# Three local edits in a seven-product block multiply: when a 2.3 MB load is issued, when one weight split stands in its queue, and which bank one product gets

## The chip, the cores and the metric

The kernel runs on one core of one Trainium2 chip. The metric is the device time of one execution in microseconds (us). Before the change the median of three runs is 2394.07 us (2391.72 to 2394.24). The engines are named as in the profile: PE multiplies matrices, PEld is its weight load, DVE is the vector engine, ACT the scalar engine, POOL is GpSimd, and SP issues most of the DMAs. The built program holds one list of instructions for each engine, with waits on semaphores that the others raise; the trace shows each list carried out in its order.

## The reference, cut to what matters

One layer of an encoder trunk is computed for 512 prompt frames and 64 sample frames, so 576 columns, which the kernel handles as two halves of 288 columns:

```python
proj = rmsnorm(x) @ w_in                  # 2048 -> 6144: q, k, v, gb, gc, hc
o_attn = stick_breaking(q, k, v)          # 8 heads
o_conv = gb * conv3(gc * hc)              # 1024 channels, 8 groups of 128
x = x + concat(rmsnorm(o_attn), rmsnorm(o_conv)) @ w_out
x = x + (silu(h2 @ w_gate) * (h2 @ w_up)) @ w_down     # h2 = rmsnorm(x); 5632 wide
```

Everything is in float32. The kernel multiplies in a rounded form (fp32r), so each operand is split into a high part and a low part, and each product is made of three matmuls: high x high, low x high and high x low, with the weights' part named first.

## The kernel before, in words

**Seven products.** Most of the large multiplies are blocked two by two: the inner dimension in even and odd chunks, the output channels in two groups c = 0, 1, the frames in two halves i = 0, 1. The four output blocks (c, i) come from seven products instead of eight, numbered 1 to 7 here as in the code, written (n, p) for product p of unit n. Each product is 24 matmuls of 128x288 (8 chunks by three). The sums and differences of weights that the products need are made by DVE in place, those of the frames beforehand: for products 5, 6, 7 and 4 of the convolution's units they lie in DRAM as `xs_dram[0..3]`. Products 1, 6, 5 and 3 of a unit accumulate one after another in one PSUM bank (`psy`), 7 and 4 in another (`psw`), and 2 has its own (`psx`). What is in `psy` after product 1, 6 and 5 is needed by itself, so ACT copies it out each time (`kept`, L1591 in the units of the second part, L1044 in the first) before the next product may go on adding to the bank. Block (1, 1) is `psw` after product 7 plus the copy after product 5; block (0, 1) is `psy` after product 3; block (1, 0) is `psw` after product 4 plus the copy after product 6.

**The order.** PE's order is written out by hand in two lists. `corder` (L1155) is for the convolution's units and the attention's share of the output projection: it begins (0,1), (0,2), (1,1), (1,2), (0,7), (0,6), (0,5), (0,3), (0,4), (1,6), (1,7), (1,5), and then (2,1), (1,3), (1,4). `order` (L1502) is for the gate, up and down units: it begins (0,1), (0,2), (1,1), (1,2), (0,6), (0,7), (0,5), (0,3), (0,4). So in the first list unit 0 already differs from the others, and there the fifth product of unit 0 has a bank of its own (L1083 to L1091): ACT copies it out (L1088), POOL adds the earlier copy to it (L1090), DVE makes block (1, 1) from `psw` and that sum (L1059, then a multiply by the row scale R, L1061), and block (0, 1) is `psy` plus the copied fifth product.

**Weights.** `conv_prepare(n, p)` (L975) makes one product's weights: DVE forms the sum if one is due (L993, L997, L1006, L1010, L1011), ACT writes the high part (L1004, 128x1024), DVE subtracts it for the low part (L1007, 128x1024). In the second part `prepare` does the same with the helper at L223 and L224, and the sums at L1526 to L1532. Four weight buffers are in turn, so a product's weights can be made up to four products ahead. `begin` (L1171) says after which products of `corder` the first weights are prepared: the entry with index k_ lists the places in `corder` whose weights are made after place k_ has run. Up to place 8 the orders of ACT and DVE are those of the program text; behind it, a scheduler of the tile framework orders them when the program is built.

**Loads at the start of the convolution's units.** SP's queue carries, in this order: the stores of the attention's forms (`form_dram<-hf`, L553), the eight loads of `xs_dram[0]` into the tiles `x` (L1152, 288 KB each), one load of weight columns (`raw_a`, L970, called from `conv_prepare` once a place is free: it holds the second column group of unit 1), the load of `xs_dram[3]` into `xs_t` (`load_sum`, L861, 2304 KB, called after place 2 of `corder`), and two more loads of weight columns. The tile of `xs_t` takes the memory of `hf`. `xs_t` is what product (0,4) multiplies; the sums for products 6 and 7 were loaded earlier, `x` serves product 5.

**Evictions.** `conv_run` (L1039) runs a product and then lets DVE make what blocks are complete: after product 2, `done` (L1047) adds the copy of product 1 to `psx` (L1059) and multiplies by R (L1061). Product 2 of units 0 and 1 use one bank, `z0`. In the second part `run` (L1585) and `finish` (L1394) do the same for gate and up: an add (L1404), a multiply by R (L1405), and for the gate a Silu on ACT (L1407); a block without an added part takes the multiply alone (L1402).

Of the kernel before, what the change touches and what calls it, by code (L numbers as in the profile page):

```python
# [10 lines left out]
F32 = mybir.dt.float32  # L11
F32R = mybir.dt.float32r
AF = mybir.ActivationFunctionType
ALU = mybir.AluOpType
PSUM = bass.MemoryType.PSUM

P = 128
# [3 lines left out]
HALF = T // 2  # L21
# [73 lines left out]
def tile_hybrid_stream_step(  # L95
# [6 lines left out]
    nc = tc.nc  # L102
# [14 lines left out]
    tmp = ctx.enter_context(tc.tile_pool(name="tmp", bufs=2, side="left"))  # L117
# [63 lines left out]
    def load_weight():  # L181
        i = len(raws)
        raws[i], raw3, src = weight_raw(i)
        nc.sync.dma_start(out=raw3, in_=src)

    def split_weight(lo_eng):
        raw = raws[len(ready)]
        n = specs[len(ready)][1] * specs[len(ready)][2]
        hi, lo = weight_split(len(ready))
        for a in range(0, n, 1024):  # L190
            weight_parts(raw, hi, lo, a, a + 1024, lo_eng)
# [69 lines left out]
    def misc(name):  # L261
        return ps_z.tile([P, 512], F32, tag="misc", name=name, bufs=2)
# [111 lines left out]
    with tc.manual_schedule(engines={mybir.EngineType.Activation, mybir.EngineType.DVE, mybir.EngineType.SP}):  # L374
# [26 lines left out]
        for kt in range(KD + LAG):  # L401
# [21 lines left out]
            if kt == 16:  # L423
                nc.vector.tensor_tensor(out=lo1[:, :1024], in0=raws[1][:, :1024], in1=hi1[:, :1024].bitcast(F32),  # L424
                                        op=ALU.subtract)
# [58 lines left out]
    for i in range(5):  # L484
        n = P if i < 4 else TS
# [373 lines left out]
    def load_sum(q):  # L859
        t = bt[q] = bt["pool"].tile([P, NP, 2, HALF], F32R, tag=f"t{q}", name=f"xs_t{q}")  # L860
        nc.sync.dma_start(out=t.bitcast(F32), in_=xs_dram[q].rearrange("j f p t -> p j f t"))  # L861

    def open_units():
        cx = apool.tile([P, 1024 + UW + 2 * HALF], F32, tag="ob", name="cx")
        bt["mx"] = cx[:, 1024 + UW :].rearrange("p (f t) -> p f t", t=HALF).bitcast(F32R)
        bt["s1"] = cx[:, :1024].rearrange("p (j c) -> p j c", c=P)
        bt["c"] = cx[:, 1024 : 1024 + UW - 2]
# [239 lines left out]
    def load_forms(tile_, at, f):  # L1107
        ft[f] = tile_[:, at : at + NH // 2]
        nc.sync.dma_start(out=ft[f].bitcast(F32), in_=form_dram[f - 1].rearrange("j f p t -> p j f t"))

    def open_out():

        xpool.release()
        bt["y"] = ypool = tc.alloc_tile_pool(name="ypool", bufs=1, reuse_waits="tile", side="right")
        x2t.extend(ypool.tile([P, 2, T], F32, tag=f"y{j}", name=f"x2_{j}") for j in range(NP))
        bt["m"] = tc.alloc_tile_pool(name="mpool", bufs=1, reuse_waits="tile", side="right")
        bt["mc"] = bt["m"].tile([P, 2, NG, 2, HALF], F32R, name="mixc")
        bt["R"] = rpool.tile([P, T], F32, tag="R", name="R_c", bufs=2)
        pipe.spawn(load_rest())
        pipe.spawn(state_out())  # L1120
        pipe.spawn(group_scale(bt["acc"], bt["R"], 7), 7 * 28)
# [6 lines left out]
    def add_x(d):  # L1128
        nc.gpsimd.dma_start(out=x2t[d], in_=xt_dram[2 * d : 2 * d + 2].rearrange("k p t -> p k t"), accum_op=ALU.add)
# [21 lines left out]
    for j in range(NP):  # L1151
        nc.sync.dma_start(out=xt[j][:, 0, 1].bitcast(F32), in_=xs_dram[0, j].rearrange("f p t -> p f t"))  # L1152
    pipe.flush()
    open_units()
    corder = [(0, 1), (0, 2), (1, 1), (1, 2), (0, 7), (0, 6), (0, 5), (0, 3), (0, 4), (1, 6), (1, 7), (1, 5)]  # L1155
    for n in range(2, len(CU)):
# [11 lines left out]
            corder += [(n, 1), (n - 1, 3), (n - 1, 4), (n, 2), (n, 6), (n, 7), (n, 5)]  # L1168


    begin = [(), (3, 4), (5,), (6, 7), (8,), (), (9,), (10, 11), (12,)]  # L1171
    turn_mode = ExitStack()
    for k_, (n, p_) in enumerate(corder):
        if (n, p_) == (NCU - 1, 1):
            turn_mode.enter_context(tc.manual_schedule(engines={mybir.EngineType.SP}))
        if k_ == len(begin) - 1:
            start_mode.close()
        conv_run(n, p_)
        for q in begin[k_] if k_ < len(begin) else range(k_ + 4, min(k_ + 5, len(corder))):
            conv_prepare(*corder[q])  # L1180
        if k_ == 2:
            load_sum(3)
        if n == NCU - 1 and p_ in (6, 7, 4):
            q = {6: 1, 7: 2, 4: 3}[p_]
            t = bt["pool"].tile([P, NH, 2, HALF], F32R, tag=f"t{q}", name=f"forms{q}")
            for at, f in enumerate({1: (1, 2), 2: (6, 7), 3: (5, 3)}[q]):
                load_forms(t, 4 * at, f)
            if p_ == 7:
                load_forms(apool.tile([P, NH // 2, 2, HALF], F32R, tag="oa", name="forms0"), 0, 4)
        if (n, p_) == (NCU - 1, 3):  # L1190
            open_out()
        if n >= NCU and p_ == (3 if n < NCU + 2 or n == len(CU) - 1 else 4):
            add_x(n - NCU)
        if k_ in (len(corder) - 10, len(corder) - 5):
            load_weight()
        if k_ == len(corder) - 4:
            split_weight(nc.vector)
# [292 lines left out]
    def frames(n, p_):  # L1490

        kind, _, a, m = UNITS[n]
        if kind == "down":
            return [(slots[a + j][p_ - 1][:, 0, :], slots[a + j][p_ - 1][:, 1, :]) for j in range(m)]
        if p_ < 3:
            return h2a[p_ - 1 :: 2]
        if p_ == 3:
            return b22s
        return [(frame_sum(p_, j, 0), frame_sum(p_, j, 1)) for j in range(m)]
# [77 lines left out]
    def multiply(ps, n, p_, start):  # L1577
        whl, xs_ = operand.pop((n, p_)), frames(n, p_)
        for j, (xh, xl) in enumerate(xs_):
            for q, (w_, x_) in enumerate(((0, xh), (1, xh), (0, xl))):  # L1580
                mm(ps, whl[:, w_, j, :], x_, start=(start and j == 0 and q == 0),  # L1581
                   stop=(j == len(xs_) - 1 and q == 2), skip_group_check=True)
            pipe.tick()

    def run(n, p_):  # L1585
        st = unit[n]
        kind, fp = UNITS[n][:2]

        def kept(tag):
            t = tmp.tile([P, HALF], F32, tag=tag, name="part", bufs=1)  # L1590
            nc.scalar.copy(out=t, in_=st["y"])  # L1591
            return t

        def done(c, i, ps, part=None):
            if kind != "down":
                finish(kind, fp, c, i, ps, part)
            elif n in last:
                store_y(n, c, i)

        def add(c, i, ps, part=None):  # L1600

            if kind != "down":
                return
            if n in first:
                if part is not None:
                    nc.vector.tensor_tensor(out=acc[fp, c, i], in0=ps, in1=part, op=ALU.add)
                else:
                    nc.scalar.copy(out=acc[fp, c, i], in_=ps)
                return
            if ps is not None:  # L1610
                nc.vector.tensor_tensor(out=acc[fp, c, i], in0=ps, in1=acc[fp, c, i], op=ALU.add)
            if part is not None:
                nc.gpsimd.tensor_tensor(out=acc[fp, c, i], in0=acc[fp, c, i], in1=part, op=ALU.add)

        if kind == "down" and p_ == 1 and n in first:
            take_blocks(fp)
        later = n not in first
        if p_ == 1:
            st["y"] = ps_pj.tile([P, HALF], F32, tag="pj", name="psy")
            multiply(st["y"], n, 1, True)  # L1620
            st["p1"] = kept("ms")
        elif p_ == 2:
            x = ps_z.tile([P, 512], F32, tag="z0", name="psx2")[:, :HALF]
            multiply(x, n, 2, True)
            add(0, 0, x, st["p1"])
            done(0, 0, x, st["p1"])
        elif p_ == 6:
            multiply(st["y"], n, 6, False)
            st["u2"] = kept("ms" if n == NGU - 1 else "t")
            if later:  # L1630
                add(1, 0, None, st["u2"])
        elif p_ == 7:
            st["w"] = ps_z.tile([P, 512], F32, tag=f"z{n % 2 + 1}", name="psw")[:, :HALF]
            multiply(st["w"], n, 7, True)
            if later:
                add(1, 1, st["w"])
        elif p_ == 5:
            multiply(st["y"], n, 5, False)
            u4 = kept("acc")
            add(1, 1, None if later else st["w"], u4)  # L1640
            done(1, 1, st["w"], u4)
        elif p_ == 3:
            multiply(st["y"], n, 3, False)
            add(0, 1, st["y"])
            done(0, 1, st["y"])
        else:
            multiply(st["w"], n, 4, False)
            add(1, 0, st["w"], None if later else st["u2"])
            done(1, 0, st["w"], st["u2"])
# [6 lines left out]
    for d, v in visits.items():  # L1656
        n = next(a for a, b in zip(v, v[1:]) if a >= NGU + 10 and b >= a + 4)
        residual.setdefault(n + 1, []).append(d)
    acc = {}
# [190 lines left out]
```

## Time and profile before

| | us |
|---|---|
| median of three runs | 2394.07 (2391.72 to 2394.24) |
| the profiled execution, device time | 2392.95 |
| its span, first to last instruction | 2391.2 |
| PE busy in the span | 2368.7 |
| DVE busy | 1902.1 |
| ACT busy | 1165.2 |
| POOL busy | 289.1 |

All times below are counted from the start of the span; what lies around it is 2392.95 - 2391.2 = 1.75 us. A row of the timeline gives the start, the duration, the engine, the line of the kernel, the operation, the output and its inputs, and the count of instructions that were merged; in square brackets stands how long the engine had been idle before, and what released it. A row of 24 matmuls is one product. Durations of matmul rows contain a tail of about 0.16 us that overlaps the next row, so products are best counted from start to start. A row of the waits says who waited for whom, the total, how often, and the longest. A row of the windows gives a stretch, its length, each engine's busy time and number of instructions, the granted share of PE's clock, the busy share of the DMA engines, and GB/s. A row of DMA issues gives the queue, the count, the size of each, and the median time from issue to landing.

### The profile page before, as it was taken

To read this page: it belongs to the slowest core of one execution; us is meant where nothing else is said; L and a number is where in the kernel's file an instruction comes from. 1 tells how busy PE (TensorE), PEld (TensorE's weight loads), DVE (VectorE), ACT (ScalarE), POOL (GpSimd) and SP (SyncE) were. 2 spreads that over 40 slices of the span, in tenths; PEclk is the share of its full clock that TensorE was granted. 3 is DMA by queue.
4 is the path that set the end of the run, shared out by engine and by line. 5 is a ranking of instruction groups with operands and counts; after the bars stand their busy time and mean duration, and the time that the engine had idled before them with its cause. 6 is when DMAs were issued, how large, how long until landed. Compare 5 with 4: busy or idle time off the path is not lost.

```text
span 2391.2 us, 44089 instructions
## 1 busy us (share of the span) xinstructions
PE 2368.7 (99%) x17813; PEld 2358.7 (99%) x17813; DVE 1902.1 (80%) x2855; ACT 1165.2 (49%) x2087; POOL 289.1 (12%) x385
## 2 busy tenths in 40 slices
PE   8999999999999999999999999999999999999999
PEld 8999999999999999999999999999999999999998
DVE  7867776688887768888888888888888777977875
ACT  6666665444444545444444444444444444444444
POOL 1111111241121120000000000000000002431211
PEclk9999999999999999999999999999999999999999
DMA  7354433584367643435534534434444935885642
GB/s 256 116 149 144 144 112 96 190 278 126 108 215 199 206 138 116 145 119 156 157 110 156 160 114 157 151 123 148 151 132 145 342 130 197 227 233 197 201 132 81
DMA packets 503764, 386.04 MB, mean 161 GB/s; under 512 B 11534, under 2 KB 492680, under 8 KB 503560
## 3 DMA queue, kind: packets, MB, share of 16 engines
q1 hardware_dynamic: 494216, 366.68, 47.9%
q0 software_dynamic: 8624, 16.22, 3.3%
q8 instruction: 139, 2.28, 0.4%
q14 instruction: 65, 0.53, 0.1%
q10 hardware_dynamic: 720, 0.33, 0.0%
HBM read 296.47 MB, written 86.72 MB: 160 GB/s over the span
## 4 chain that ended last, share of the span: by engine, by line
PE 90%; DVE 4%; DMA 3%; ACT 2%; issue 1%; POOL 0%; SPq 0%; ACTq 0%; DVEq 0%; POOLq 0%
PE psy L1581 34%; PE psw L1581 17%; PE pj L214 11%; PE psx L1581 8%; PE psy L1035 6%; PE pjo L214 4%; PE psw L1035 3%; PE pw L1424 2%; PE psx L1035 1%; DMA raw_a<-in_w_out_dram 1%; PE z L684 1%; DMA xs_t<-xs_dram 1%; PE po L751 0%; DVE wlo L177 0%; DVE whl L1007 0%
## 5 line engine op out<-in xcount | busy, mean ns | idle before, releaser
L1581 PE MATMUL psy<-t,whl 128*128 128x288 f32 x2916 | 438.0, 295 | 0.0
L1581 PE MATMUL psy<-h_s,whl 128*128 128x288 f32 x2724 | 410.9, 294 | 0.0
L1581 PEld LDWEIGHTS psy<-t,whl 128*128 128x128 f32 x2916 | 403.4, 188 | 0.0
L214 PE MATMUL pj<-x,whi 128*128 128x288 f32 x1856 | 398.9, 299 | 0.3 <-DVE x L357 0.3
L1581 PEld LDWEIGHTS psy<-h_s,whl 128*128 128x128 f32 x2724 | 377.9, 188 | 0.3 <-ACT part L1591 0.3
L1581 PE MATMUL psw<-t,whl 128*128 128x288 f32 x2592 | 377.0, 295 | 0.0
L224 DVE TENSOR_TENSOR whl<-raw_a,whl 128x1024 fp32r<-128x1024 f32 (+4 forms) x288 | 313.4, 1089 | 58.9 <-ACT whl L223 57.9
L1581 PEld LDWEIGHTS psw<-t,whl 128*128 128x128 f32 x2592 | 354.1, 188 | 0.0
L223 ACT CAST whl<-raw_a 128x1024 fp32r<-128x1024 f32 (+4 forms) x288 | 259.5, 902 | 118.1 <-issue 35.4
L214 PEld LDWEIGHTS pj<-x,whi 128*128 128x128 f32 x1856 | 307.3, 189 | 1.0 <-DVE x L357 0.6
L214 PE MATMUL pj<-x,wlo 128*128 128x288 f32 x928 | 274.5, 296 | 0.1
L224 DVE TENSOR_TENSOR whl<-raw_b,whl 128x1024 fp32r<-128x1024 f32 (+5 forms) x186 | 194.4, 1045 | 69.7 <-ACT whl L223 68.5
L223 ACT CAST whl<-raw_b 128x1024 fp32r<-128x1024 f32 (+5 forms) x186 | 161.0, 868 | 162.1 <-issue 69.9
L1591 ACT COPY part<-psy 128x288 f32<-128x288 f32 x237 | 94.5, 399 | 272.5 <-PE psy L1581 271.3
L214 PEld LDWEIGHTS pj<-x,wlo 128*128 128x128 f32 x928 | 175.2, 189 | 0.7 <-DVE wlo L424 0.3
L1581 PE MATMUL psx<-h_s,whl 128*128 128x288 f32 x1122 | 165.0, 295 | 0.0
L1581 PEld LDWEIGHTS psx<-h_s,whl 128*128 128x128 f32 x1122 | 154.1, 188 | 0.0
L1339 POOL DMA_DIRECT2D hid_dram<-form x3 | 2.2, 748 | 975.7 <-DVE form L224 975.7
L223 ACT CAST whl<-s 128x1024 fp32r<-128x1024 f32 (+5 forms) x79 | 70.1, 888 | 98.9 <-PE psw L1581 97.3
L177 DVE TENSOR_TENSOR wlo<-raw_a,whi 128x1024 fp32r<-128x1024 f32 (+1 forms) x80 | 96.6, 1224 | 10.1 <-ACT whi L176 8.0
L214 PE MATMUL pjo<-mixc,whi 128*128 128x288 f32 x512 | 101.7, 294 | 0.0
L176 ACT CAST whi<-raw_a 128x1024 fp32r<-128x1024 f32 (+1 forms) x85 | 85.6, 1024 | 29.4 <-PE pj L214 15.6
(469 smaller groups left out, 4114.9 us busy)
## 6 DMA issues: line engine op xcount, KB each, us to landing
hid_dram<-form SPq DMA_DIRECT2D x146, 288.0 KB, 2.3
raw_a<-in_w_in_dram SPq DMA_DIRECT2D x41, 1024.0 KB, 6.9
raw_a<-in_w_gate_dram SPq DMA_DIRECT2D x23, 1024.0 KB, 5.9
raw_a<-in_w_up_dram SPq DMA_DIRECT2D x23, 1024.0 KB, 5.9
raw_b<-in_w_gate_dram SPq DMA_DIRECT2D x21, 1024.0 KB, 6.7
raw_b<-in_w_up_dram SPq DMA_DIRECT2D x21, 1024.0 KB, 7.5
h_s<-hid_dram SPq DMA_DIRECT2D x10, 2016.0 KB, 8.5
raw_a<-in_w_out_dram SPq DMA_DIRECT2D x16, 1024.0 KB, 5.2
```

Source lines behind the costliest of these rows:

```text
L176: nc.scalar.copy(out=hi[:, a:b], in_=raw[:, a:b])
L177: lo_eng.tensor_tensor(out=lo[:, a:b], in0=raw[:, a:b], in1=hi[:, a:b].bitcast(F32), op=ALU.subtract)
L214: mm(ps, w_[:, k, csl], x_, start=(k == 0 and n == 0), stop=(k == nk - 1 and n == 2))
L223: nc.scalar.copy(out=hi, in_=src)
L224: (lo_eng or nc.vector).tensor_tensor(out=lo, in0=src, in1=hi.bitcast(F32), op=ALU.subtract)
L684: mm(zb[i], a_[:, kk], b_[:, q0:TP], start=(n == 0), stop=False, skip_group_check=True)
L1035: mm(ps, whl[:, w_, j, :], x_, start=(start and j == 0 and q == 0), stop=(j == m - 1 and q == 2), skip_group_check=True)
L1339: q.dma_start(out=hid_dram[fp][2 * n - 2 : 2 * n].rearrange("f p t -> p f t"), in_=t.bitcast(F32))
L1424: mm(pss[j, i], w_[:, k, j * P : (j + 1) * P], x_, start=(kk == 0 and k == 0 and n == 0), stop=(kk == 1 and k == 7 and n == 2))
L1581: mm(ps, whl[:, w_, j, :], x_, start=(start and j == 0 and q == 0), stop=(j == len(xs_) - 1 and q == 2), skip_group_check=True)
L1591: nc.scalar.copy(out=t, in_=st["y"])
```

## The change: what it does

- `load_sum(3)`, the load of `xs_dram[3]` into `xs_t`, is called before the units begin, directly behind the eight loads of `xs_dram[0]`, instead of after place 2 of `corder`.
- The weights of (1,2), place 3 of `corder`, are prepared after product (0,1) instead of after (0,2), so their split stands ahead of the eviction of (0,2) in the queues. Those of (0,7) stay where they were.
- In the first gate unit (unit 0 of the second part) the fifth product gets a bank of its own. ACT copies it out, POOL adds the copy of product 6 to it for block (1, 1), and block (0, 1) is `psy` plus the copied fifth product.

```diff
     pipe.flush()
+    load_sum(3)
     open_units()
...
-    begin = [(), (3, 4), (5,), (6, 7), (8,), (), (9,), (10, 11), (12,)]
+    begin = [(3,), (4,), (5,), (6, 7), (8,), (), (9,), (10, 11), (12,)]
...
         for q in begin[k_] if k_ < len(begin) else range(k_ + 4, min(k_ + 5, len(corder))):
             conv_prepare(*corder[q])
-        if k_ == 2:
-            load_sum(3)
...
+        elif p_ == 5 and n == 0:
+
+            x = misc("psx5")[:, :HALF]
+            multiply(x, n, 5, True)
+            st["p5"] = tmp.tile([P, HALF], F32, tag="acc", name="part5", bufs=1)
+            nc.scalar.copy(out=st["p5"], in_=x)
+            u4 = tmp.tile([P, HALF], F32, tag="ms", name="part", bufs=1)
+            nc.gpsimd.tensor_tensor(out=u4, in0=st["p5"], in1=st["u2"], op=ALU.add)
+            done(1, 1, st["w"], u4)
         elif p_ == 5:
             multiply(st["y"], n, 5, False)
...
         elif p_ == 3:
             multiply(st["y"], n, 3, False)
             add(0, 1, st["y"])
-            done(0, 1, st["y"])
+            done(0, 1, st["y"], st.get("p5"))
```

When the two programs are built, every engine's instructions stand in the same order up to the start of the convolution's units. From there, on SP `xs_t` moves ahead of one `raw_a` load. On DVE the L1007 of (1,2) moves ahead of the L1059 and L1061 of (0,2). Behind place 8 the scheduler's order of DVE and ACT differs in some places up to the middle of the units: above all, both evictions that belong to (0,3) and (0,4) stand directly behind the low part of (1,6), and on ACT the copy of (1,6) and the convolution's first tap (L890) stand ahead of the high part of (1,5). In the gate unit one POOL add, one DVE add and other names are the only differences.

## The prediction

> **What bounds the kernel now.** I read the totals first, then what PE waited for, then the timeline at those waits.
>
> ```profile
> PE 2368.7 (99%) x17813; PEld 2358.7 (99%) x17813; DVE 1902.1 (80%) x2855; ACT 1165.2 (49%) x2087; POOL 289.1 (12%) x385
> ...
> PE psw L1035 <- DMA xs_t<-xs_dram: 3.4, 1, 3.4
> ...
> PE psy L1581 <- ACT part L1591: 1.4, 1, 1.4
> ...
> PE psx L1035 <- DVE whl L1007: 0.9, 1, 0.9
> ```
>
> PE is busy 99% of 2391.2 us; only what shortens its few waits can help. Each edit aims at one of these three: 5.7 us together. The first costs more than its wait:
>
> ```profile
> 513.26 1.22 DVE L1007 TENSOR_TENSOR whl<-raw_a,whl 128x1024 fp32r<-128x1024 f32 x1
> 514.54 3.07 PEld L1035 LDWEIGHTS psw<-xs_t,whl 128*128 128x128 f32 x23 [0.37 <-DVE whl L1007]
> ...
> 520.86 3.33 PE L1035 MATMUL psx<-x,whl 128*128 128x288 f32 x24
> 524.03 3.33 PE L1035 MATMUL psy<-x,whl 128*128 128x288 f32 x24
> 530.73 4.95 PE L1035 MATMUL psw<-xs_t,whl 128*128 128x288 f32 x24 [3.37 <-DMA xs_t<-xs_dram]
> 535.52 3.37 PE L1035 MATMUL psy<-xs_t,whl 128*128 128x288 f32 x24
> 528.00:532.00 4.00, 1.27 (x6) 1.30 (x7) 2.80 (x4) 1.99 (x2) 0.00 (x0) 0.87 1.12 361
> 532.00:536.00 4.00, 4.00 (x24) 4.00 (x23) 2.09 (x5) 0.24 (x1) 1.39 (x2) 0.71 0.15 43
> ```
>
> The first two rows are the low part of (0,7) and PE's weight loads waiting for it; the PE rows below are (0,5), (0,3), (0,4), (1,6). A product takes 3.17 us start to start (520.86 to 524.03). From (0,3) to (1,6) there are two products, 6.34, but the trace has 535.52 - 524.03 = 11.49. So the late `xs_t` costs **5.15 us**: 3.53 until (0,4) starts, and 1.62 because it then runs at a granted clock of 0.87 and 0.71.
>
> **Part 1, the load of `xs_t`: removes 5.15.**
>
> ```profile
> 506.51 4.56 SPq L1152 DMA_DIRECT2D x<-xs_dram  x8
> 518.11 0.37 SPq L970 DMA_DIRECT2D raw_a<-in_w_in_dram  x1
> 518.54 1.92 SPq L861 DMA_DIRECT2D xs_t<-xs_dram  x1
> 516.00:518.00 2.00, 2.00 (x17) 2.00 (x17) 1.97 (x2) 1.06 (x1) 0.00 (x0) 1.00 0.24 84
> 520.00:530.60 10.60, 7.36 (x56) 7.12 (x54) 6.17 (x8) 2.62 (x5) 0.80 (x1) 1.00 1.08 347
> xs_t<-xs_dram SPq DMA_DIRECT2D x1, 2304.0 KB, 12.1
> ```
>
> Before, `xs_t` stood in SP's queue behind a `raw_a` load that waited until 518.11 for DVE. Now it follows the eight `x` loads, at 506.51 + 4.56 = 511.1. Those keep the DMA engines busy until about 517 (84 GB/s in 516 to 518, so they are running dry). 2304 KB (2.36 MB) at the 347 GB/s of the busy stretch is 6.8 us, so `xs_t` lands near 523.8. (0,4) wants it at 524.03 + 3.17 = 527.2 or later: the wait and the slow clock go. The old DMA gap around 518 hides the move. Also on SP's queue, the `raw_a` of (1,6) is now behind `xs_t`: 1.05 MB more, 3.0 us, 526.8. Who needs that is below.
>
> **Part 2, the split moved up: adds 0.9.**
>
> ```profile
> 508.58 1.05 ACT L1004 CAST whl<-raw_c 128x1024 fp32r<-128x1024 f32 x1
> 508.71 0.46 DVE L1059 TENSOR_TENSOR cv<-psx,part 128x288 f32<-128x288 f32 x1
> 509.20 0.46 DVE L1061 TENSOR_TENSOR cv<-cv,R 128x288 f32<-128x288 f32 x1
> 509.66 1.23 DVE L1007 TENSOR_TENSOR whl<-raw_c,whl 128x1024 fp32r<-128x1024 f32 x1
> 510.80 1.22 DVE L993 TENSOR_TENSOR raw_a<-raw_a 128x1024 f32<-128x1024 f32 x1
> 510.94 3.33 PE L1035 MATMUL psx<-x,whl 128*128 128x288 f32 x23 [0.86 <-DVE whl L1007]
> ```
>
> (1,2) waited for its low part. That in turn started 0.03 after ACT's high part ended (508.58 + 1.05 = 509.63). ACT's order is unchanged here, so the L1007 can't start earlier; it has only moved ahead of L1059 and L1061, which used DVE while ACT was still at work. DVE now idles until 509.66, and the two follow at 510.80. Two things wait for that. (1,2) uses bank `z0`, so its first matmul waits until L1059 has read it: 510.80 + 0.46 = 511.26, some 0.5 later than now. And L993 and all behind it come later by what the pair took, 509.66 - 508.71 = 0.95, less about 0.1 of overlap: 0.9 (estimate). The first to feel it is (0,7), which already waits for its low part (0.37 above): that ends at 515.4 instead of 514.5. (0,7) thus starts its stream 0.9 later, the 0.5 included. Were ACT's cast earlier, up to the 0.86 would be won instead; nothing in ACT's order makes it so.
>
> **What is late next.** Now (1,6) wants to start at 535.52 - 5.15 + 0.9 = 531.27, and its weights have a chain of their own:
>
> ```profile
> 524.72 0.80 POOL L1090 TENSOR_TENSOR part<-part,part 128x288 f32<-128x288 f32 x1 [14.76 <-ACT part L1088]
> 525.55 0.46 DVE L1059 TENSOR_TENSOR cv<-psw,part 128x288 f32<-128x288 f32 x1 [3.20 <-POOL part L1090]
> ...
> 526.42 1.22 DVE L993 TENSOR_TENSOR raw_a<-raw_a,raw_c 128x1024 f32<-128x1024 f32 x1
> 530.06 1.23 DVE L1007 TENSOR_TENSOR whl<-cx,whl 128x1024 fp32r<-128x1024 f32 x1 [1.17 <-ACT whl L1004]
> ```
>
> It hangs on the end of (0,5), which is 0.9 later: L993 at 527.3 (its `raw_a`, at 526.8, just in time), low part at 530.95 to 532.2. The second matmul of (1,6) wants it at 531.4: **0.9 lost** (0.87 in the sum). (1,7) then wants its low part at 535.4: on DVE two evictions (four operations of 0.46 or less) and two shorter pieces stand before it, about 2 us with overlap, so it is ready at about 535.2, just in time. For (1,5), ACT's new order puts the copy of (1,6) and the tap L890 first:
>
> ```profile
> 538.73 1.22 DVE L1007 TENSOR_TENSOR whl<-raw_a,whl 128x1024 fp32r<-128x1024 f32 x1
> 538.98 0.40 ACT L1044 COPY part<-psy 128x288 f32<-128x288 f32 x1 [0.58 <-PE psy L1035]
> 540.35 0.79 ACT L890 ACTIVATE uc<-uc,vec 128x578 f32<-128x578 f32 x1
> 541.37 0.81 DVE L892 SCALAR_TENSOR_TENSOR uc<-uc,vec 128x578 f32<-128x578 f32 x1
> 541.90 9.68 PE L1035 MATMUL psy<-x,whl 128*128 128x288 f32 x72
> ```
>
> (1,6) ends at 531.27 + 0.87 + 3.17 + 0.16 = 535.5; copy to 535.9, L890 to 536.7, L892 (now ahead of L1011) to 537.5, L1011 (a 128x1024 sum like L993, 1.22) to 538.65, L1007 of (1,5) to 539.8. (1,5) wants that at 535.3 + 3.17 + 0.13 = 538.6: **1.25 lost**. Before, it was ready at 538.73 + 1.22 = 539.95, ahead of 541.90. Later products have more room: the low part of (2,1) is two operations on (0.81 and 1.22, 541.8), and its product starts at 538.5 + 1.25 + 3.17 = 542.9. Parts 1 and 2: 5.15 - 0.9 - 0.87 - 1.25 = **2.1 us won**.
>
> **Part 3, the gate unit: removes 1.7, adds 0.5.**
>
> ```profile
> 974.25 0.39 ACT L1591 COPY part<-psy 128x288 f32<-128x288 f32 x1
> 974.39 1.22 DVE L224 TENSOR_TENSOR whl<-raw_a,whl 128x1024 fp32r<-128x1024 f32 x1
> 974.69 0.67 PE L1581 MATMUL psy<-h_z,whl 128*128 128x288 f32 x3 [1.43 <-ACT part L1591]
> 975.52 0.45 DVE L1404 TENSOR_TENSOR gs<-psw,part 128x288 f32<-128x288 f32 x1
> 978.00 0.56 PE L1581 MATMUL psw<-t,whl 128*128 128x288 f32 x3
> 2018.76 0.68 DVE L224 TENSOR_TENSOR whl<-raw_a,whl 128x512 fp32r<-128x512 f32 x1
> 2018.98 2.36 POOL L1613 TENSOR_TENSOR acc<-acc,part 128x288 f32<-128x288 f32 x2 [5.02 <-issue]
> ```
>
> (0,3) waited 1.43 for the copy of (0,5), and its first matmuls dragged. With a bank of its own for (0,5) (one that nothing else uses in these units), (0,3) follows at 974.69 - 1.43 = 973.26, and (0,4) can start at 976.43 instead of 978.00: 1.57, and 1.7 with the tail of the old row (0.16, as the idle time is counted from its end). But (0,4) accumulates on `psw`, which L1404 must have read, and L1404 now waits for POOL's add. That add is 0.80 alone (the L1090 row); two of them took 2.36 where DVE ran L224 beside them, 0.76 more than 2 x 0.80. Here it falls into L224, 974.39 to 975.61. Unhindered it ends at 975.5 and L1404 is on time; held until L224 ends, it ends at 976.4, L1404 at 976.9, and (0,4) loses 0.5. I take the second, as that is what the nearest rows show. Behind L1404 on DVE stand the split of (1,7), which PE wants only after (0,4) and (1,6), so 6 us later, and the one added add (0.45), hidden there. Part 3: **1.2 us won**, between 1.0 and 1.7.
>
> The Trainium skill, "GPSIMD Engine Reference", section 8 (Key points), says that GpSimd shares its SBUF interfaces with VectorE and contends with DVE instructions that have two inputs in SBUF. L224 has two, and the 2.36 agrees; without that rule the sum would be 0.5 better.
>
> **Sum.** 2392.95 - 2.1 - 1.2 = 2389.6 us, which is 3.3 (0.14%) off the profiled execution and 4.5 below the median of the three runs; those differ by 2.5 among themselves. I predict 2389.6.
>
> **Rivals.**
> 1. *DVE keeps up.* If neither (1,6) nor (1,5) waits, parts 1 to 3 give 5.15 - 0.9 + 1.7 = 5.95: 2387.0. For it: DVE idles 3.20 before 525.55. Against: both chains start from PE's own products, so an earlier PE doesn't bring them forward. It holds if their waits sum to under 0.5.
> 2. *The columns come late: slower.* If the DMA engines mix `xs_t` with the two `raw_a` loads behind it, all 4.46 MB end near 517 + 12.9 = 529.9, and L993 waits 2.6. (1,6) then waits 3.5, about as long as the wait that cost 1.62 in clock: 2.6 + 1.6 = 4.2 lost against 3.3 won, so 2393.9. It decides from a landing at 529.8. Against: `xs_t` landed at 518.54 + 12.1 = 530.6, ahead of the last `raw_a`, so the queue goes roughly in order.
> 3. *The moved split does what it says:* (1,2) no longer waits and nothing is lost behind it: 0.9 + 0.86 better, 2387.8. Against: ACT's row at 508.58.
>
> The Trainium skill, "TensorE: Matmul & The Clock Gate", Part 1, puts the idle window after which the clock is halved at about 3.4 us. The waits of 3.53 and 0.86 agree (the shorter one left full speed); by it rival 2 would pay the clock's 1.6 only above that.
>
> **How the numbers follow.** Forecast 0.62; rival 1 0.18; rival 2 0.10 (its price is mostly under 0.2%); rival 3 0.06; other 0.04. A measurement of this kernel can tell about 0.2% (4.8 us) from no change; the forecast lies within that, and some of its spread, and rivals 1 and 3, beyond. Faster 0.31, same 0.64, slower 0.05. Range: from 2386.4 (rival 1 and a little) to 2393.2 (part of rival 2, and runs as high as the median before).
>
> **What would show it.** Right: no PE wait on `xs_t` and full clock at (0,4); the L1007 of (1,2) still at 509.7 with L1059 behind it; PE waits of about 1 us on DVE at (1,6) and (1,5); no wait on the copy at (0,3), and 0.5 at (0,4). Wrong: `raw_a` landing after 528, no waits at (1,6) and (1,5), or a new wait past 545.

## The result, and the profile after

| | before | after |
|---|---|---|
| median, 22 runs each | 2392.76 (2390.74 to 2396.58) | 2389.60 (2387.41 to 2391.72) |
| ratio of the times, with its 95% interval | | 0.9986 [0.9979, 0.9992] |
| span of the profiled execution | 2391.2 | 2386.8 |
| start of (1,1) to start of (1,4), convolution | 45.08 | 43.05 |
| start of (0,6) to start of (0,4), first gate unit | 14.42 | 12.69 |

The kernel became 0.14% faster, and the predicted 2389.6 was met. The gain is small, but the interval of the ratio doesn't reach 1: it allows for a gain of 0.08% to 0.21%. The two stages in which something was edited account for 2.03 + 1.73 = 3.76 of the 4.4 us between the two spans. The other 0.6 is scatter between executions: already before (1,1), where both programs are the same, the execution after stands 1.22 us earlier (505.12 against 506.34), and half of that is lost again where nothing was edited.

The busy line of the page of after, and below it what PE waited for (total, times, longest):

```profile
PE 2366.7 (99%) x17813; PEld 2356.1 (99%) x17813; DVE 1899.5 (80%) x2856; ACT 1165.2 (49%) x2087; POOL 295.5 (12%) x386
```

```profile
PE psy L1035 <- DVE whl L1007: 2.2, 3, 1.0
PE psx L1035 <- DVE cv L1059: 1.5, 1, 1.5
...
PE psw L1035 <- DVE whl L1007: 0.5, 1, 0.5
...
PE psy L1580 <- ACT part L1590: 0.2, 1, 0.2
```

Two of the three waits that the edits aimed at are gone: that for `xs_t` (3.4) and that for the copy of (0,5) (1.4; 0.2 on such a copy is left; one line came and two went above, so L1591 of before is L1590 here). The third, at (1,2), is longer than it was: 1.5 on L1059 where there were 0.9 on L1007. New are the waits for low parts at (1,6) and (1,5), the 0.7 and 1.0 within the first row.

PE's timeline of after; a row of 24 is one product, a row of 1 is a first matmul whose second one waits:

```profile
505.12 3.54 PE L1035 MATMUL psy<-x,whl 128*128 128x288 f32 x24
510.14 3.41 PE L1035 MATMUL psx<-x,whl 128*128 128x288 f32 x24 [1.48 <-DVE cv L1059]
513.39 0.29 PE L1035 MATMUL psw<-xs_t,whl 128*128 128x288 f32 x1
514.14 3.31 PE L1035 MATMUL psw<-xs_t,whl 128*128 128x288 f32 x23 [0.46 <-DVE whl L1007]
517.29 3.33 PE L1035 MATMUL psy<-xs_t,whl 128*128 128x288 f32 x24
...
526.81 3.33 PE L1035 MATMUL psw<-xs_t,whl 128*128 128x288 f32 x24
529.98 0.29 PE L1035 MATMUL psy<-xs_t,whl 128*128 128x288 f32 x1
530.95 3.35 PE L1035 MATMUL psy<-xs_t,whl 128*128 128x288 f32 x23 [0.68 <-DVE whl L1007]
534.14 3.33 PE L1035 MATMUL psw<-xs_t,whl 128*128 128x288 f32 x24
537.31 0.29 PE L1035 MATMUL psy<-x,whl 128*128 128x288 f32 x1
...
548.17 3.33 PE L1035 MATMUL psw<-xs_t,whl 128*128 128x288 f32 x24
```

The rows are (1,1), (1,2), (0,7) in two, (0,6); then (0,4) at 526.81 at full speed and without a wait, (1,6) in two, (1,7), the start of (1,5), and (1,4). From (1,1) to (0,6) the stage takes 12.17 (before 11.34), from (0,6) to (1,4) 30.88 (before 33.74). I call these two pieces the **front** and the **tail**; the front holds the cost of the moved split, the tail the gain of the load and what came late behind it. Nine products at 3.17 without a wait would make a tail of 28.5.

DVE's timeline of after, for the same places, with the one row of ACT that matters for (1,5):

```profile
508.40 1.22 DVE L1007 TENSOR_TENSOR whl<-raw_c,whl 128x1024 fp32r<-128x1024 f32 x1 [1.05 <-ACT whl L1004]
509.55 0.45 DVE L1059 TENSOR_TENSOR cv<-psx,part 128x288 f32<-128x288 f32 x1
...
526.02 1.22 DVE L993 TENSOR_TENSOR raw_a<-raw_a,raw_c 128x1024 f32<-128x1024 f32 x1
...
534.22 1.22 DVE L1010 TENSOR_TENSOR raw_a<-cx,raw_c 128x1024 f32<-128x1024 f32 x1
534.67 0.79 ACT L890 ACTIVATE uc<-uc,vec 128x578 f32<-128x578 f32 x1
535.49 0.82 DVE L892 SCALAR_TENSOR_TENSOR uc<-uc,vec 128x578 f32<-128x578 f32 x1
536.23 1.22 DVE L1011 TENSOR_TENSOR cx<-raw_c,cx 128x1024 f32<-128x1024 f32 x1
537.37 1.22 DVE L1007 TENSOR_TENSOR whl<-raw_a,whl 128x1024 fp32r<-128x1024 f32 x1
```

The moved L1007 waits 1.05 for ACT's cast, and L1059, which (1,2) needs, now stands behind it. L993 of (1,6) starts with no wait on record; L892 and L1011 stand ahead of the low part of (1,5), which ends at 538.59; (1,5) goes on at 538.64. L892 itself starts when two things have just ended, the tap L890 on ACT (535.46) and L1010 on DVE (535.44).

### The profile page after: what moved, and what is told of

It reads as the page before. It is cut to its first block, busy times and chain, and to the rows that moved or that the text cites. A ratio compares the mean times of both kernels' runs of the same rounds, so it can differ in the third digit from the quotient of the medians.

```text
span 2386.8 us, 44094 instructions
## 1 busy us (share of the span) xinstructions
PE 2366.7 (99%) x17813; PEld 2356.1 (99%) x17813; DVE 1899.5 (80%) x2856; ACT 1165.2 (49%) x2087; POOL 295.5 (12%) x386
## 4 chain that ended last, share of the span: by engine, by line
PE 87%; DVE 6%; DMA 3%; ACT 2%; issue 1%; POOL 1%; SPq 0%; ACTq 0%; DVEq 0%; POOLq 0%
PE psy L1580 32%; PE psw L1580 16%; PE pj L214 11%; PE psx L1580 8%; PE psy L1035 6%; PE pjo L214 4%; PE psw L1035 3%; PE pw L1423 2%; PE psx L1035 1%; DMA raw_a<-in_w_out_dram 1%; DMA raw_a<-in_w_down_dram 1%; DVE whl L224 1%; PE z L684 1%; PE po L751 0%; DVE whl L1007 0%
## 5 line engine op out<-in xcount | busy, mean ns | idle before, releaser
L224 DVE TENSOR_TENSOR whl<-raw_a,whl 128x1024 fp32r<-128x1024 f32 (+4 forms) x288 | 312.9, 1087 | 61.3 <-ACT whl L223 60.6
L224 DVE TENSOR_TENSOR whl<-raw_b,whl 128x1024 fp32r<-128x1024 f32 (+5 forms) x186 | 194.4, 1045 | 70.0 <-ACT whl L223 69.0
L1590 ACT COPY part<-psy 128x288 f32<-128x288 f32 x236 | 94.1, 399 | 273.7 <-PE psy L1580 273.5
```

Of the source, the lines that this page charges most:

```text
L224: (lo_eng or nc.vector).tensor_tensor(out=lo, in0=src, in1=hi.bitcast(F32), op=ALU.subtract)
```

## The experiments

There are twelve experiments. Nine were executed 11 times, and the median is given; the others have one execution. The kernels were timed in three groups, and those of a group share the runs of the kernel before (medians 2392.86, 2393.32 and 2393.07). Stage times are from each kernel's one profiled execution, start to start, so they and the median need not agree.

| run | front | tail | gate (0,6) to (0,4) | median, us below before |
|---|---|---|---|---|
| before | 11.34 | 33.74 | 14.42 | |
| the change | 12.17 | 30.88 | 12.69 | 3.16 |
| e1, load only | 11.36 | 33.53 | 14.57 | 2.10 |
| e2, split only | 12.21 | 33.98 | 14.14 | -0.89 |
| e3, bank only | 11.35 | 33.72 | 12.69 | 2.34 |
| e4, load and bank | 11.35 | 32.07 | 13.42 | 3.34 |
| e5, e4 with two half loads | 11.38 | 30.83 | 13.48 | 4.08 |
| e6, the change, tap later | 13.13 | 31.13 | 12.69 | 1.76 |
| e7, e5 with early sum, tap later | 11.36 | 29.59 | 13.34 | 4.64 |
| e8, the change again | 12.50 | 30.85 | 13.49 | 2.62 |
| e9, e5 with early sum | 12.09 | 29.55 | 13.23 | one run |
| e10, e9 with the sum on DVE | 11.35 | 29.57 | 12.69 | 5.22 |
| e11, e1 again | 11.43 | 33.62 | 14.37 | one run |
| e12, e4 again | 11.58 | 31.53 | 13.45 | one run |

In e6, e8, e9 and e12 the front also holds a wait within (1,1) itself (0.86, 0.28, 0.70, 0.21), where the programs are the same: scatter.

### Each part alone, and the two that looked good together

Each part of the change is run by itself, then two of them together, each run with a theory and a rival of its own.

**e1**, the load alone:

```diff
     pipe.flush()
+    load_sum(3)
     open_units()
...
-        if k_ == 2:
-            load_sum(3)
```

> Only the load of xs_t is moved. Theory (each edit has its own price, and half of the load's gain is given back): no PE wait on xs_t, new PE waits on DVE of about 0.7 at (1,6) and 1.0 to 1.2 at (1,5), because their chains start from PE's own products. From (1,1) to (1,4), 45.08 us start to start before and 43.05 with all edits, it gives 42.2, and the run is 2.9 us faster than before. Rival (DVE as a whole limits this stretch, so what the moved split costs would be waited for anyway): 43.0, as with all edits, 2.0 faster.

Measured: 2390.76 (2388.4 to 2394.09), ratio 0.9992 [0.9984, 1.0001]. In the profile nearly all of the gain of the load is gone: front and tail together take 44.89, against the theory's 42.2 and the rival's 43.0, so both fail there. The median, 2.10 below before, is what the rival gave; but the profiled execution, 2393.49, is among the longest of the eleven, 2.73 above their median, so its rows needn't stand for the others. PE's rows of (1,6) in e1, and a stretch with its granted clock (the number behind POOL's busy time):

```profile
530.30 0.40 PE L1035 MATMUL psy<-xs_t,whl 128*128 128x288 f32 x1 [0.70 <-ACT whl L1004]
531.56 4.84 PE L1035 MATMUL psy<-xs_t,whl 128*128 128x288 f32 x23 [0.86 <-DVE whl L1007]
```

```profile
532.00:536.00 4.00, 4.00 (x21) 4.00 (x21) 4.00 (x8) 0.15 (x1) 1.62 (x2) 0.60 0.00 0
```

(1,6) waits twice, 0.70 and 0.86, and then runs at a clock of 0.60, so 23 matmuls take 4.84 where 24 took 3.33 elsewhere. What made the wait longer than in the change is seen best in e4.

**e2**, the split alone (the `begin` line of the change, nothing else):

> Only the split of (1,2) is moved. Theory: L1007 of (1,2) starts no earlier after PE's products than before, L1059 and L1061 follow it, (0,7) comes 0.8 to 0.9 later, and as the load of xs_t hangs on DVE's L1011, the wait for it is as long as before: from (1,1) to (1,4) 45.9 (45.08 before), 0.8 us slower. Rival (the split does what it says): the 0.86 at (1,2) goes, 44.2, 0.9 faster. Second rival (hidden by the wait for xs_t behind it): 45.1.

Measured: 2393.75 (2391.64 to 2396.75), ratio 1.0006 [0.9997, 1.0015]. The front is 0.87 longer; front and tail take 46.19, 0.3 more than the theory's 45.9. Theory met; both rivals are out, the one by which the split does what it says (44.2) and the one by which the wait for `xs_t` hides its cost (45.1; that wait is 3.63 here). In the profile the split alone thus costs at least 0.9; the median, 0.89 above before, agrees, but its interval also holds a ratio of 1.

**e3**, the bank of the gate unit alone (the last two pieces of the change's diff):

> Only the first gate unit's fifth product has its own bank. From (0,6) to (0,4) of that unit it is 14.42 start to start before, 12.69 with all edits. Theory: POOL's add is lengthened by DVE's split to about 1.4, but ACT's copy comes early enough: 12.7, 1.7 us faster. Rival (the prediction's step): the copy stands behind ACT's cast by 0.9 as before, and (0,4) waits 0.5 for L1403: 13.2, 1.2 faster.

Measured: 2390.52 (2390.08 to 2395.08), ratio 0.9992 [0.9983, 1.0001]. (0,6) to (0,4) takes 12.69, with no wait at (0,4): 1.73 less than in the profile of before, where the prediction had taken 1.2. The section on the gate unit below shows that the two profiles are not alike there, and that 1.73 is therefore too much for the bank alone.

**e4**, load and bank, without the split:

> The change without its moved split. Theory: from (1,1) to (1,4) 42.2, from (0,6) to (0,4) of the gate unit 12.7, so 2.9 + 1.7 = 4.6 us faster than before (2388.2 against 2392.8) and 0.8 to 0.9 faster than the change. Rival (DVE limits the stretch anyway): 43.0 and 12.7, the same as the change, 3.7 faster than before.

Measured: 2389.52 (2386.94 to 2392.51), ratio 0.9986 [0.9977, 0.9995]. Front and tail take 43.42, above the theory's 42.2 and the rival's 43.0, although the front is the short one. DVE and PE at (1,6) in e4:

```profile
525.89 1.22 DVE L993 TENSOR_TENSOR raw_a<-raw_a,raw_c 128x1024 f32<-128x1024 f32 x1 [1.16 <-DMA raw_a<-in_w_in_dram]
```

```profile
529.57 0.40 PE L1035 MATMUL psy<-xs_t,whl 128*128 128x288 f32 x1 [0.79 <-ACT whl L1004]
530.83 3.33 PE L1035 MATMUL psy<-xs_t,whl 128*128 128x288 f32 x23 [0.87 <-DVE whl L1007]
```

L993 waits 1.16 for its weight columns (1.07 in e1), so the `raw_a` load behind `xs_t` comes late after all, and (1,6) waits 1.66 in two pieces. In the change L993 starts without a wait: 20.90 after the start of (1,1), against 21.32 here and 21.24 in e1. The moved split delays DVE by about what the columns are late, so behind the load it costs next to nothing: 43.05 and 43.35 with it (the change and e8), 43.42 and 43.11 without (e4 and e12). That is what the rival gave, but the cause is the load's order and not DVE's work. In the gate unit (0,4) waits 0.57 here, as the prediction had it.

### What holds (1,6), and what holds (1,5)

From here the theory is: L993 starts at the later of two things, the end of (0,5)'s eviction and the landing of `raw_a`; and (1,5) waits for what stands ahead of its split on DVE.

**e5**, e4 with the load of `xs_t` cut in two halves, the second behind the `raw_a` of (1,6):

```diff
     pipe.flush()
+    load_sum(3, 0, NP // 2)
     open_units()
...
         if k_ == 2:
-            load_sum(3)
+            load_sum(3, NP // 2, NP)
```

> Parts 1 and 3 without the moved split, but the load of xs_t is cut in two: chunks 0 to 3 behind the x loads, chunks 4 to 7 at the old place, behind the raw_a of (1,6). Theory (two gates): L993 of (1,6) starts at the later of two things, the end of (0,5)'s eviction and the landing of raw_a, and in the run with parts 1 and 3 the landing came last (DVE idled 1.16 for it). With half of xs_t (1.18 MB, 3.0 us at 392 GB/s) behind it, raw_a lands near 522.9 on that run's clock of times, L993 follows L1061 without a wait, 1.16 earlier; the waits of (1,6) fall from 1.66 to 0.8 to 0.9; (1,1) to (1,4) takes 42.3 to 42.7 instead of 43.42, and (0,4) doesn't wait for the second half. Rival (the DMA engines mix what is outstanding): raw_a lands no earlier, L993 still waits about 1.1, (1,1) to (1,4) stays at 43.4. Median: theory 2388.6, rival 2389.5.

Measured: 2389.24 (2387.25 to 2392.23), ratio 0.9985 [0.9976, 0.9994]; front and tail 42.21. DVE and PE in e5 (its lines are one higher, so L1062 and L994 are L1061 and L993 above):

```profile
526.82 0.46 DVE L1062 TENSOR_TENSOR cv<-cv,R 128x288 f32<-128x288 f32 x1
527.19 1.22 DVE L994 TENSOR_TENSOR raw_a<-raw_a,raw_c 128x1024 f32<-128x1024 f32 x1
```

```profile
532.12 3.31 PE L1036 MATMUL psy<-xs_t,whl 128*128 128x288 f32 x23 [0.68 <-DVE whl L1008]
```

The sum follows the eviction with no wait, and (1,6) waits 0.68. The theory is met in the profile; the median lies between the theory's 2388.6 and the rival's 2389.5 and doesn't decide. What stands ahead of the columns in SP's queue decides when they land: the rival, in which the DMA engines mix the loads, is out. With the columns in time, the short front (11.38) and the short tail (30.83, as in the change) come together, 0.84 better than the change. I read that as the price of the moved split once nothing hides it; no run has the two half loads together with the split.

**e6**, the change, with the end of group 0 called one product later:

```diff
-            if kind == "u":
+            if kind == "u" and n:
                 end_u(g)
...
             conv_prepare(*corder[q])
+        if k_ == 9:
+            end_u(CU[0][1])
```

> The whole change, and the end of group 0 (L887 to L892: the copies of the state on POOL, the tap L890 on ACT, the two L892 on DVE) is called one product later, behind (1,6). Theory: (1,5) waited 1.04 because L890 and one L892 stood ahead of its split; now its low part is ready about 0.8 to 1.2 earlier, the wait at (1,5) is at most 0.3, (1,5) to (1,4) takes 9.5 to 9.8 instead of 10.86, (1,1) to (1,4) 41.8 to 42.0 instead of 43.05, median 2388.4. Rival: what holds (1,5) is the chain from (1,7)'s low part through L1010, so the wait stays at 0.7 or more and (1,1) to (1,4) at 42.7 to 43.1; or the tap comes late for group 1 and a new wait stands behind (1,4). Median then 2389.6.

Measured: 2391.56 (2386.86 to 2392.45), ratio 0.9990 [0.9981, 0.9998]; (1,5) waits 1.31, more than before this edit. The theory's numbers failed; the rival's wait of 0.7 or more is met. DVE in e6:

```profile
537.27 1.22 DVE L1010 TENSOR_TENSOR raw_a<-cx,raw_c 128x1024 f32<-128x1024 f32 x1
538.41 1.22 DVE L1007 TENSOR_TENSOR whl<-raw_a,whl 128x1024 fp32r<-128x1024 f32 x1
539.54 1.22 DVE L1011 TENSOR_TENSOR cx<-raw_c,cx 128x1024 f32<-128x1024 f32 x1
540.68 1.22 DVE L1007 TENSOR_TENSOR whl<-raw_a,whl 128x1024 fp32r<-128x1024 f32 x1
```

The scheduler put the low part of (2,1) (538.41) where L892 had stood; that is 0.4 longer (1.22 against 0.82), and (1,5), whose own low part is the row at 540.68, waits 0.27 longer. So the run didn't test what it was made for, and it doesn't decide between theory and rival; but here too what stands ahead on DVE is what (1,5) waits for. On ACT, L890 ends at 538.50 and L1010 on DVE at 538.49, so the high part of (1,5), at 538.52, couldn't have started earlier without the tap.

**e7**, e5 with the tap later, and with the sum L993 of (1,6) ahead of (0,5)'s eviction:

```diff
-            tt(out=a21, in0=a21, in1=a11, op=ALU.subtract)
+            if n != 1:
+                tt(out=a21, in0=a21, in1=a11, op=ALU.subtract)
...
+        if k_ == 6:
+            nc.vector.tensor_tensor(out=cregion[1, 1][1], in0=cregion[1, 1][1], in1=cregion[1, 0][1], op=ALU.subtract)
         conv_run(n, p_)
```

> Parts 1 and 3 without the moved split, xs_t in two loads as in the run before the last, the end of group 0 called one product later, and the sum L993 of (1,6) placed on DVE ahead of (0,5)'s eviction. Theory: raw_a lands near 522.9 on the clock of times of the run with parts 1 and 3, L993 runs until 524.1, the eviction of (0,5) ends 0.3 later than there, which (0,4) doesn't feel; the split of (1,6) is 0.7 to 0.8 earlier than with the two loads alone, its wait at most 0.2, the wait at (1,5) at most 0.3; (1,1) to (1,4) takes 40.2 to 40.8, and with the gate unit's 1.2 to 1.7 the median is near 2387.0. Rival: the landing of raw_a now holds DVE ahead of (0,5)'s eviction, and (0,4), which sums on the same bank, waits 0.5 to 2 for it: (1,1) to (1,4) 41.5 to 43, median 2388.5 to 2389.5.

Measured: 2388.68 (2385.6 to 2392.51), ratio 0.9979 [0.9971, 0.9988]; front and tail 40.95, 0.15 above the theory's upper end, the median 1.7 above its number. (1,6) waits 0.38, (1,5) to (1,4) takes 9.87, where before it was 9.52 and in the change 10.86, and (0,4) isn't held, so the rival is out. In this profile the landing was less early than reckoned: 18.96 after (1,1), against 21.2 to 21.3 for the whole load ahead of it, so 2.3 instead of 3.0.

**e9**, e7 without the later tap:

> As the run with the early sum and the later tap, but the end of group 0 is called where it was. Theory: it is the place of the operations in DVE's order that frees (1,5), and that order comes from the early sum alone; the later call of the tap did nothing. (0,6) to (1,4) takes 29.4 to 29.9 as there (29.59), with no wait at (1,5). Rival: the later call did it: (1,5) waits 0.7 or more and it takes 30.3 to 30.9.

Measured: 2386.09 (one run), tail 29.55. PE's row of (1,5) to (1,3) in e9:

```profile
535.78 10.04 PE L1037 MATMUL psy<-x,whl 128*128 128x288 f32 x72
```

Before, 72 such matmuls took 9.68 without a wait, so the row still holds a short one. From (1,5) to (1,4) it is 9.87, as in e7: of the 1.34 that the change loses there (10.86 against 9.52), 0.35 is left. Theory met, except that the wait is not quite gone: the early sum did it, through the order that the scheduler then made, in which only a multiply by R and L1011 stand between L1010 and the split of (1,5). From the start of (1,6)'s low part to the end of (1,5)'s DVE now takes 7.93 instead of the 8.92 of the change; L892 (0.82) and one L882 (0.45), which overlap their neighbours a little, no longer stand between. The later tap did nothing.

**e11**, e1 again:

> The load alone once more. L993 of (1,6) waits for raw_a about 1.1, and (1,6) waits about 1.6 in two pieces. Theory: that the PE clock fell to 0.5 behind these two pieces in the first run of it (24 matmuls in 4.84 instead of 3.33) was chance, as the run with parts 1 and 3 had the same pieces at full clock: (0,6) to (1,4) takes 32.0 to 32.2, with the clock at 1.0. Rival: the lone load always pays the clock: 33.4 to 33.6.

Measured: 2395.28 (one run), tail 33.62. The number is the rival's: L993 waits 1.18, (1,6) waits 0.81 and 0.86, and the clock is down to 0.57 again (534 to 538). In e4 the same two waits (0.79 and 0.87) left it at 1.0. Why, the runs don't settle: two profiles with a drop and one without are too few, and the two programs are the same up to the gate unit. That the lone load always pays the clock isn't shown: the median of e1, 2.1 below before, and its profiled execution, 2.73 above that median, speak for executions that kept the clock (1.7 less by the tail of e4), but none was profiled.

**e12**, e4 again:

> Parts 1 and 3 once more. Theory: L993 of (1,6) waits 1.0 to 1.2 for raw_a again, (1,6) waits 1.5 to 1.7, (0,6) to (1,4) takes 32.0 to 32.2 (33.5 if the clock falls). In the gate unit (0,6) to (0,4) takes 12.7 if the cast of the form waits about 2 us for the write of the forms and 13.4 if it waits over 3. Rival: the 1.16 was scatter of one run; L993 waits under 0.5, and the stage takes 31.0 to 31.6.

Measured: 2391.12 (one run), tail 31.53. L993 waits 0.57, between the theory's 1.0 and the rival's 0.5; (1,6) waits 0.21 and 0.86. The landing of `raw_a` scatters by half a microsecond between executions, and with it this stage; the 43.42 of e4 has that uncertainty. The gate unit took 13.45 at a wait for the write of 3.39, as expected.

### The gate unit: two phases

**e8**, the changed kernel again:

> The changed kernel once more, for the gate unit and for the scatter. Theory: whether (0,4) of the gate unit waits depends on when the write of the forms to DRAM ahead of it lands, which holds ACT and with it the copy of (0,5): if the cast of the form waits about 2.0 us for that write, as in the first profile of the change, (0,4) doesn't wait and (0,6) to (0,4) takes 12.7; if it waits about 3.3, as before the change and with parts 1 and 3, ACT's cast stands ahead of the copy, (0,4) waits about 0.6 and it takes 13.4. Rival: the gate unit takes 12.7 whatever that wait, and 13.4 needs another cause. (1,1) to (1,4) takes 43.0 to 43.4 by both. Median 2389.6.

Measured: 2390.70 (2388.46 to 2393.12), ratio 0.9988 [0.9979, 0.9997]; (0,6) to (0,4) takes 13.49. The first profile of the change, then e8, ACT, DVE, POOL and PE around (0,3):

```profile
953.32 0.43 ACT L223 CAST form<-ut 128x288 fp32r<-128x288 f32 x1 [1.97 <-DMA hid_dram<-form]
...
969.79 0.55 PE L1580 MATMUL psy<-h_z,whl 128*128 128x288 f32 x3
969.99 0.40 ACT L1641 COPY part<-psx 128x288 f32<-128x288 f32 x1
970.04 1.23 DVE L224 TENSOR_TENSOR whl<-raw_a,whl 128x1024 fp32r<-128x1024 f32 x1
970.47 1.46 POOL L1643 TENSOR_TENSOR part<-part,part 128x288 f32<-128x288 f32 x1 [69.88 <-ACT part L1641]
971.96 0.46 DVE L1403 TENSOR_TENSOR gs<-psw,part 128x288 f32<-128x288 f32 x1 [0.70 <-POOL part L1643]
```

```profile
956.37 0.43 ACT L223 CAST form<-ut 128x288 fp32r<-128x288 f32 x1 [3.91 <-DMA hid_dram<-form]
...
971.37 0.56 PE L1580 MATMUL psy<-h_z,whl 128*128 128x288 f32 x3
971.73 1.05 ACT L223 CAST whl<-raw_a 128x1024 fp32r<-128x1024 f32 x1 [3.40 <-DVE raw_a L1529]
972.68 0.39 ACT L1641 COPY part<-psx 128x288 f32<-128x288 f32 x1
972.82 1.22 DVE L224 TENSOR_TENSOR whl<-raw_a,whl 128x1024 fp32r<-128x1024 f32 x1
973.15 1.55 POOL L1643 TENSOR_TENSOR part<-part,part 128x288 f32<-128x288 f32 x1 [71.45 <-ACT part L1641]
974.73 0.46 DVE L1403 TENSOR_TENSOR gs<-psw,part 128x288 f32<-128x288 f32 x1 [0.70 <-POOL part L1643]
...
975.34 1.85 PE L1580 MATMUL psw<-t,whl 128*128 128x288 f32 x12 [0.63 <-DVE gs L1403]
```

In the first, the cast of a form waits 1.97 for a write to DRAM, ACT copies (0,5) 0.20 after (0,3) begins, and L1403 ends at 972.42, before (0,4) is due at 972.96. In the second it waits 3.91, ACT is later against PE, a cast of weights stands ahead of the copy, which comes 1.31 after (0,3) begins, and (0,4) waits 0.63. All ten runs with the bank fall in two groups by that wait: 1.97, 2.12, 2.15 and 2.16 gave 12.69 each time; 3.17, 3.27, 3.36, 3.39, 3.91 and 4.37 gave 13.23, 13.34, 13.42, 13.45, 13.49 and 13.48. Theory met. Why the write lands at two times isn't known from these runs.

The gate unit without the bank has the two phases too. ACT and PE in e2, which has the old gate unit:

```profile
957.25 0.43 ACT L223 CAST form<-ut 128x288 fp32r<-128x288 f32 x1 [2.32 <-DMA hid_dram<-form]
974.39 0.66 PE L1581 MATMUL psy<-h_z,whl 128*128 128x288 f32 x3 [1.18 <-ACT part L1591]
```

The write held the cast for 2.32 there, and (0,6) to (0,4) took 14.14; before, e11 and e1 had 3.27, 3.25 and 4.33 and took 14.42, 14.37 and 14.57. So the 1.73 compares a late execution of before with an early one of after. Like against like the bank wins 14.14 - 12.69 = 1.45 in the early phase (one profile without the bank) and 0.9 to 1.3 in the late one (14.37 to 14.57 against 13.23 to 13.49).

**e10**, e9 with the gate unit's new sum on DVE:

```diff
-            nc.gpsimd.tensor_tensor(out=u4, in0=st["p5"], in1=st["u2"], op=ALU.add)
+            nc.vector.tensor_tensor(out=u4, in0=st["p5"], in1=st["u2"], op=ALU.add)
```

> As the run before, and the added sum of the gate unit (u4, the copy of (0,5) plus the copy of (0,6)) on DVE instead of POOL. Theory: (0,4) of the gate unit waited 0.5 to 0.6 in runs in which ACT's copy came late, because POOL's add took 1.5 beside DVE's L224 and L1403 (by its line in the changed kernel) behind it; on DVE the add takes 0.45, so (0,4) doesn't wait (at most 0.1) wherever the copy falls, and (0,6) to (0,4) takes 12.7 to 12.8. Rival: the add now stands on DVE behind L224 and in front of the splits, (0,4) still waits 0.3 or more, or a later product waits as much. Median: theory 2388.0, rival 2388.6.

Measured: 2387.85 (2385.83 to 2389.4), ratio 0.9979 [0.9970, 0.9988]; gate unit 12.69, no wait at (0,4) nor at the products behind it. But the write landed early (2.16), where POOL's sum didn't hold (0,4) either, so whether DVE's sum helps in the late case stays open. DVE in e10 (L1409 is L1403 of the change):

```profile
967.70 1.22 DVE L224 TENSOR_TENSOR whl<-raw_a,whl 128x1024 fp32r<-128x1024 f32 x1
968.84 0.45 DVE L1649 TENSOR_TENSOR part<-part,part 128x288 f32<-128x288 f32 x1
969.33 0.46 DVE L1409 TENSOR_TENSOR gs<-psw,part 128x288 f32<-128x288 f32 x1
```

L1409 ends at 969.79, 0.87 ahead of (0,4) at 970.66; in the change that lead was 972.96 - 972.42 = 0.54. This is the lowest median measured: 5.22 us (0.21%) below before, against 2.62 to 3.16 for the change. Its interval overlaps those of e7 and of the change.

## Why the prediction was right, point by point

- **The late `xs_t` costs 5.15, and the load removes it: right.** Without the split, (0,4) runs at full speed and without a wait in e1, e4, e5.
- **The moved split adds 0.9: right** for the front (0.83 in the change, 0.87 in e2), but not as what the edit costs beside the load. By the prediction's terms the change without it should have won 5.15 - 0.87 - 1.25 = 3.0 in these units; e4 won 1.66 and e12 1.97. What the prediction didn't see: the columns of (1,6) are so late that DVE would have waited 0.6 to 1.2 anyway. It had called them "just in time" *with* the split, which is what the change's profile shows (L993 20.90 after (1,1), forecast 527.3 - 506.34 = 20.96); it did not ask what they would be without it. So the late columns of its rival 2 are there in e1, e4, e11 and e12, at a quarter to a half of the 2.6 it was priced at; but they come from the loads' order, as e5 shows, and not from the mixing that the rival named.
- **(1,6) loses 0.87, (1,5) 1.25: right.** (1,6) to (1,7) took 4.16 instead of 3.21, so 0.95 more, and (1,5) to (1,4) 10.86 instead of 9.52, 1.34 more. For (1,5) the named chain, the copy of (1,6), L890, L892, L1011, L1007, is in the trace, but it is half of the matter: DVE's own work up to L1010 ends at the same time as the tap (535.44 and 535.46), so an earlier tap alone would have changed nothing. What matters is that L892 stands ahead of the split on DVE: in e9 it no longer does, and 0.35 of the 1.34 is left. Rival 1 (DVE keeps up) is out.
- **Parts 1 and 2 together, 2.1 won:** 2.03 in the first profile, 1.73 in e8.
- **Part 3, 1.2 won: right, like against like.** POOL's sum was slow every time, 1.42 to 1.56 beside L224 against 0.80 alone, as the Trainium skill, "GPSIMD Engine Reference", section 8, would have it. But the step "held until L224 ends, it ends at 976.4 ... and (0,4) loses 0.5" was taken as the one value, and it is one of two: whether (0,4) feels the slow sum depends on when the copy ahead of it comes. The trace of before was of the late phase (its cast waited 3.27), and there the 0.5 is about right (0.54 to 0.80 lost in six runs); in the other phase nothing is lost. The bank's gain of 0.9 to 1.3 in the late phase and 1.45 in the early one lies about the forecast, mostly inside the range named, 1.0 to 1.7; the 1.73 read off the first two profiles holds a change of phase.
- **The sum.** 3.3 was forecast. The two profiles of the change give 3.76 and 2.66, the medians 3.16 and 2.62: the forecast stands between the profiles and 0.1 to 0.7 above the medians. Since the gate unit alone moves by 0.8 between executions and the columns' landing by 0.5, meeting 2389.6 to the tenth is luck; meeting it within 1 us isn't, as each stage of the change came out near its forecast.

## What to carry to other kernels

When a load is moved ahead in a queue, ask what now stands behind it, and not only whether the mover comes in time: of the 5.15 that this load gave, some 3.5 were lost again to what became late next, 1.2 of them to the load behind it in the queue, and cutting it in two gave those back. An edit that is a loss alone can be free beside another one (the split behind the late columns), so take changes apart before keeping all of them. When a forecast hangs on which of two instructions comes first, one profile shows only one of the phases; look for the wait that sets the phase, price both, and compare before and after in the same phase.

## What the runs showed of the hardware that was not expected

In these traces a POOL add and a DVE operation on two tiles in SBUF hold each other up, and the one that comes second pays. In the gate unit L224 began first and kept its 1.22 while POOL's sum took 1.42 to 1.56 instead of 0.80. With the early sum of e9 POOL began first; POOL, then DVE in e9 (L1182 is the early sum, 1.22 elsewhere):

```profile
523.13 0.80 POOL L1092 TENSOR_TENSOR part<-part,part 128x288 f32<-128x288 f32 x1 [14.79 <-ACT part L1090]
```

```profile
523.16 1.86 DVE L1182 TENSOR_TENSOR raw_a<-raw_a,raw_c 128x1024 f32<-128x1024 f32 x1 [2.42 <-DMA raw_a<-in_w_in_dram]
```

POOL kept its 0.80 and DVE took 0.64 more than 1.22, for 0.77 of overlap; in e10 it was 1.70 (0.48 more) for 0.62, in e7 1.32 (0.10 more) for 0.23. So most of a long overlap is lost, and less than half of the short one.

PE's clock fell after much shorter waits than the 3.53 of before: in e1 to 0.60 and in e11 to 0.57 (means over 4 us), after two waits of 0.70 to 0.86 with one matmul between them, at a cost of 1.5 us. The Trainium skill, "TensorE: Matmul & The Clock Gate", Part 1, ties the drop to an idle window of about 3.4 us; these two profiles don't agree, while e4, with waits of the same length, kept full speed.
